# Products of two k tiles by turns, with weights at eight sets of places, and two raw weight buffers in place of three

## The chip, the core and the metric

The kernel runs on one core of one Trainium2 chip. The metric is the device time of a launch in microseconds (us). The time before is 2691.24 us, the median of 2 runs (2691.05 to 2691.44).

## What is computed

One inference step of a two-layer decoder, for a prompt of 256 tokens and 8 sequences of 8 new tokens each, 320 tokens in all, in float32. Layer 0 mixes tokens by gated linear attention (GLA), layer 1 by a chunked spatial gate; each is followed by a dense MLP with squared ReLU, and each sublayer by a residual LayerNorm:

```python
def sq_relu_mlp(x, w1, w2):
    return jnp.square(jax.nn.relu(x @ w1)) @ w2

for i in range(DEPTH):                     # DEPTH = 2
    if i % N_MIXERS == 0:
        h, s = gla_mixer(x, gla_w_in[j], ..., gla_w_out[j], gla_state0[j])
    else:
        h, v_rows = sg_mixer(x, sg_w_in[j], ..., sg_w_out[j])
    x = layer_norm(DEEPNORM_ALPHA * x + h, ln1_g[i], ln1_b[i])
    x = layer_norm(DEEPNORM_ALPHA * x + sq_relu_mlp(x, mlp_w1[i], mlp_w2[i]), ln2_g[i], ln2_b[i])
```

D_MODEL is 2048 and the MLP is 8192 wide. Nearly all the work is in the large products: `gla_w_in` (2048 x 6144 and a narrow gate part), `gla_w_out`, `sg_w_in`, `sg_w_out`, and for each layer `mlp_w1` and `mlp_w2`.

## The kernel before

**Three products for one.** Activations lie with the feature on the partition and the 320 tokens along it. A float32 operand is split in a high part, which is its value in the type float32r, and a low part, which is the rest. A weight tile w times an activation tile x becomes three TensorE products into one PSUM tile: low weights by high x (line 161), high weights by low x (L162), high weights by high x (L163). Each loads 128x128 weights and streams 320 columns (322 for a normalised input that carries two extra columns; those tiles are called dgh and dgl). The pairs of activation tiles are called xh/xl, oh/ol, yh/yl and hh/hl by stage.

**Units.** Weights come in units of 4 k tiles by 256 columns (512 KB), 736 in all. For a unit, `unit` issues a load into one of three buffers of the pool wraw (L138, on SyncE's queue, SP), lets ScalarE cast it into a high buffer wh (L144, ACT), and VectorE subtract to get the low buffer wl (L145, DVE). The first two units are loaded and split in pieces of one or two k tiles. The buffers wh and wl are taken in turn from a ring: ring a has four of each; from the end of the GLA layer on a ring b with four more of each joins, and units take the rings by turns. A unit's subtraction is what gives the raw buffer free; the last product of a unit gives its wh and wl free.

**Order of products.** `group` holds one PSUM tile for each 128 output columns, and for each unit does for both column halves n and the four k tiles kk the three products of `mm3`, in the order L161, L162, L163. The program is written in this order, and the scheduler of the tile framework then places the instructions of each engine by its own estimate of when they can start; small products of other work (attention heads, means) go in between.

**Places.** LINE is 64 floats, 256 bytes. The pools and a few unused fill tiles are laid out so that all wh tiles start at a multiple of 256 bytes in the partition; a gap tile of LINE // 4 floats (`Ring.part`) puts the wl tiles 64 bytes past one; and the big activation tiles start LINE // 2 floats, 128 bytes, into a line (`bigtile`). A row of a weight unit is 1024 bytes and a half of it 512, and a k tile of 320 activations is 1280 bytes, so these places within 256 bytes are the same for each k tile and each half. Only the dgh and dgl tiles, with 322 columns, have a different place for each k tile.

**The start.** The input x is loaded in pieces (L225, half of a quarter at a time, xr) on the same SP queue as the weights; the loads of the gate's weights (L293 into wgr, L296 into wgr2) stand there too. The narrow gate product of the GLA layer is L316 and L317: for each k tile one weight tile, taken twice, by xl and by xh. Its 16 weight tiles follow each other in steps of 512 bytes.

## Time and profile before

| | |
|---|---|
| median of the timed runs | 2691.24 us |
| profiled execution, first to last instruction (span) | 2689.4 us |
| TensorE clock granted, mean | 1.000 of full |
| DMA, mean over the span | 165 GB/s, 442.42 MB |
| weight loads on SP's queue | 512 KB each, 3.5 to 4.5 us from issue to landing in the median |
| SP's queue waiting for a raw buffer (L138 <- DVE wl L145) | 2150.6 us, 692 times |

The profile names an engine, the line of the kernel, the tiles (out<-in, buffer numbers left out), the number of instructions, then the busy time, the mean duration of one in ns, and the idle time of the engine before them with what ended it. PE is TensorE, PEld its weight loads. Matmuls overlap in the records: one of 128x320 lasts some 300 ns there, while the next starts much earlier, so the busy share of TensorE says little, and the distance from start to start is what counts. Durations of a stretch are given as min/median/max where a single line is asked for.

### The profile page before, as it was taken

What the parts mean: (1) busy time and instruction counts of PE and PEld (TensorE: products, weight loads), DVE (VectorE), ACT (ScalarE), POOL (GpSimd) and SP (SyncE); (2) the same over time, 40 slices, a digit from 0 to 9 for tenths busy, and PEclk for the clock granted to TensorE, in tenths of its full rate; (3) what the DMA queues carried; (4) which work ended last, traced back from release to release, by engine and by line L of the source; (5) the groups of instructions that cost most, each with busy time, mean ns of one, the idle gap of its engine ahead of it and who ended that gap; (6) DMA issues with size and microseconds to landing.
All of it is one profiled execution on the core that took longest, in us unless ns stands there. A gap on an engine that the chain in (4) does not pass through costs nothing.

```text
span 2689.4 us, 44906 instructions
## 1 busy us (share of the span) xinstructions
PE 2680.7 (100%) x18395; PEld 2658.8 (99%) x18395; DVE 1550.3 (58%) x2322; ACT 1162.5 (43%) x1638; POOL 226.4 (8%) x391
## 2 busy tenths in 40 slices
PE   9999999999999999999999999999999999999999
PEld 9999999999999999999999999999999999999998
DVE  7677677885444444444478776686444444444446
ACT  5455455564334334333446554355334333333434
POOL 4353341000000000000001032000000000000000
PEclk9999999999999999999999999999999999999999
DMA  8667667545445545444445555455445444454552
GB/s 252 220 196 249 217 198 253 189 142 159 155 150 155 151 150 156 150 153 152 150 152 161 157 158 149 134 165 153 153 150 156 150 152 154 150 155 150 152 154 79
DMA packets 138494, 442.42 MB, mean 165 GB/s; under 512 B 20912, under 2 KB 27952, under 8 KB 138288
## 3 DMA queue, kind: packets, MB, share of 16 engines
q1 hardware_dynamic: 121440, 408.08, 49.2%
q0 software_dynamic: 16304, 30.82, 3.7%
q8 instruction: 144, 2.36, 0.4%
q10 hardware_dynamic: 544, 0.66, 0.1%
q14 instruction: 62, 0.51, 0.1%
HBM read 409.60 MB, written 22.02 MB: 160 GB/s over the span
## 4 chain that ended last, share of the span: by engine, by line
PE 99%; DMA 0%; ACT 0%; DVE 0%; ACTq 0%; issue 0%; DVEq 0%
PE mm L161 32%; PE mm L163 32%; PE mm L162 31%; PE gl L631 1%; PE gl L634 1%; PE gl L589 1%; PE gl L1003 0%; PE gl L573 0%; DMA raw<-gla_w_in 0%; ACT z L1087 0%; DMA xr<-xT 0%; PE gl L558 0%; PE gl L603 0%; PE gl L574 0%; PE gl L552 0%; PE gl L1004 0%
## 5 line engine op out<-in xcount | busy, mean ns | idle before, releaser
L145 DVE TENSOR_TENSOR wl<-raw,wh 128x1024 fp32r<-128x1024 f32 (+1 forms) x740 | 902.3, 1220 | 953.2 <-ACT wh L144 950.9
L144 ACT CAST wh<-raw 128x1024 fp32r<-128x1024 f32 (+1 forms) x740 | 771.5, 1044 | 1251.9 <-PE mm L163 1127.1
L163 PE MATMUL mm<-yh,wh 128*128 128x320 f32 x2624 | 805.9, 307 | 0.0
L161 PE MATMUL mm<-yh,wl 128*128 128x320 f32 x2624 | 803.2, 309 | 0.0
L162 PE MATMUL mm<-yl,wh 128*128 128x320 f32 x2624 | 794.9, 303 | 0.0
L161 PE MATMUL mm<-hh,wl 128*128 128x320 f32 x2048 | 631.5, 308 | 0.0
L163 PE MATMUL mm<-hh,wh 128*128 128x320 f32 x2048 | 629.0, 307 | 0.0
L162 PE MATMUL mm<-hl,wh 128*128 128x320 f32 x2048 | 619.9, 303 | 0.0
L162 PEld LDWEIGHTS mm<-yl,wh 128*128 128x128 f32 x2624 | 492.7, 188 | 0.0
L163 PEld LDWEIGHTS mm<-yh,wh 128*128 128x128 f32 x2624 | 491.4, 187 | 0.0
L161 PEld LDWEIGHTS mm<-yh,wl 128*128 128x128 f32 x2624 | 491.0, 188 | 0.0
L161 PEld LDWEIGHTS mm<-hh,wl 128*128 128x128 f32 x2048 | 384.6, 188 | 0.0
L162 PEld LDWEIGHTS mm<-hl,wh 128*128 128x128 f32 x2048 | 384.6, 188 | 0.0
L163 PEld LDWEIGHTS mm<-hh,wh 128*128 128x128 f32 x2048 | 383.4, 187 | 0.0
L161 PE MATMUL mm<-xh,wl 128*128 128x320 f32 x768 | 238.2, 311 | 1.4 <-DVE wl L145 0.7
L163 PE MATMUL mm<-xh,wh 128*128 128x320 f32 x768 | 236.4, 309 | 0.0
L162 PE MATMUL mm<-xl,wh 128*128 128x320 f32 x768 | 235.2, 306 | 0.0
L161 PEld LDWEIGHTS mm<-xh,wl 128*128 128x128 f32 x768 | 144.1, 188 | 5.4 <-DVE wl L145 1.0
L162 PEld LDWEIGHTS mm<-xl,wh 128*128 128x128 f32 x768 | 144.3, 188 | 4.4 <-issue 1.2
L163 PEld LDWEIGHTS mm<-xh,wh 128*128 128x128 f32 x768 | 143.7, 187 | 2.6 <-issue 0.7
L1053 POOL CAST ident_r<-ident 128x128 fp32r<-128x128 f32 x1 | 0.3, 286 | 1027.9 <-PE gl L772 1027.9
L936 POOL DMA_DIRECT2D bsp<-sg_wT x1 | 0.6, 558 | 999.7 <-PE mm L163 999.7
(265 smaller groups left out, 2380.3 us busy)
## 6 DMA issues: line engine op xcount, KB each, us to landing
raw<-mlp_w SPq DMA_DIRECT2D x512, 512.0 KB, 3.5
raw<-gla_w_in SPq DMA_DIRECT2D x94, 512.0 KB, 4.1
raw<-sg_w_in SPq DMA_DIRECT2D x64, 512.0 KB, 3.6
st<-state SPq DMA_DIRECT2D x32, 512.0 KB, 5.7
o_state_s<-st POOLq DMA_DIRECT2D x32, 512.0 KB, 4.2
raw<-gla_w_out SPq DMA_DIRECT2D x32, 512.0 KB, 4.5
raw<-sg_w_out SPq DMA_DIRECT2D x32, 512.0 KB, 3.5
va<-blk POOLq DMA_DIRECT2D x128, 32.0 KB, 4.3
```

Source lines behind the costliest of these rows:

```text
L144: nc.scalar.copy(hi[:, ks, :], raw[:, ks, :])
L145: nc.vector.tensor_sub(lo[:, ks, :], raw[:, ks, :], hi[:, ks, :].bitcast(F32))
L161: nc.tensor.matmul(ps, wl[:, kk, s], x_h, start=first, stop=False)
L162: nc.tensor.matmul(ps, wh[:, kk, s], x_l, start=False, stop=False)
L163: nc.tensor.matmul(ps, wh[:, kk, s], x_h, start=False, stop=last)
L589: nc.tensor.matmul(pairs(pu), hd.ktp[:, kt, blk, :], hd.v_prompt(blk), start=(blk == 0), stop=(blk == 1))
L631: nc.tensor.matmul(po[:], qm[:, kt, b * P : (b + 1) * P], part[:], start=False, stop=(b == DB - 1 and kt == 1 and part is sth))
L634: nc.tensor.matmul(pairs(pu), kz[:, i, kt, g, :], hd.v_sample(g), start=True, stop=True)
L936: nc.gpsimd.dma_start(wsT, A["sg_wT"])
L1053: nc.gpsimd.tensor_copy(ident_r[:], ident[:])
```

## The change

`Ring.part` and `mm3` go. A new class `Weights` is a tile with its own map from k tile to offset: even k tiles start at one place in a line, odd ones at another. High and low tiles each get LINE more floats. `Ring.parts` gives the buffers of a ring, four in turn, one of four sets of places and an order of products; with two rings there are eight. `Q` is LINE // 4 floats, 64 bytes; `at(even, odd)` takes the two places in units of Q. An order is a list of six products for an even and an odd k tile: (0 or 1 for the k tile, "lh" for low weights by high x, "hl" for high weights by low x, "hh" for both high). The pool wraw has two buffers. Casts and subtractions write two runs of 512 floats for a whole unit instead of one of 1024.

```diff
+class Weights:
+    def __init__(self, tile, base, a, b):
+        self.tile, self.base, self.a, self.b = tile, base, a, b
+    def row(self, k):
+        return self.base + k // 2 * self.a + k % 2 * self.b
+    def put(self, ks):
+        k, n = ks.start, ks.stop - ks.start
+        if n == 1:
+            return self.tile[:, self.row(k) : self.row(k) + UN].rearrange("p (a b n) -> p a b n", a=1, b=1)
+        one = self.tile[:, self.row(k) : self.row(k) + 1]
+        return bass.AP(tensor=one.tensor, offset=one.offset,
+                       ap=[list(one.ap[0]), [self.a, n // 2], [self.b, 2], [1, UN]])
...
+Q = LINE // 4
+TURNS = ((0, "lh"), (0, "hl"), (1, "hl"), (1, "lh"), (1, "hh"), (0, "hh"))
+TURNS_LAST = ((0, "lh"), (0, "hl"), (1, "hl"), (0, "hh"), (1, "hh"), (1, "lh"))
+SWAPPED = tuple((1 - k, p) for k, p in TURNS)
+PLAIN = tuple((k, p) for k in range(2) for p in ("lh", "hl", "hh"))
+BOTH_LOW = ((0, "lh"), (0, "hl"), (1, "lh"), (1, "hl"), (0, "hh"), (1, "hh"))
+def at(even, odd):
+    return even * Q, UN, 2 * UN + (odd - even) % 4 * Q
+PLACES = {
+    "a": [(at(0, 1), at(1, 0), TURNS), (at(0, 3), at(3, 0), TURNS),
+          (at(0, 1), at(1, 0), TURNS_LAST), (at(0, 0), at(1, 1), PLAIN)],
+    "b": [(at(0, 3), at(1, 0), TURNS), (at(3, 0), at(0, 3), SWAPPED),
+          (at(0, 0), at(1, 1), BOTH_LOW), (at(1, 0), at(0, 1), SWAPPED)],
+}
 class Ring:
...
-        t = self.pool.tile([P, UK, UN], F32R, tag=p + self.tag, name=name)
-        if not self.gap:
-            self.pool.tile([P, LINE // 4], F32, tag="gap", name=name + "_gap", bufs=1)
-            self.gap = True
-        return t
+    def parts(self, hi, lo):
+        *at, order = PLACES[self.tag][self.turn % 4]
+        self.turn += 1
+        h, l = (Weights(self.pool.tile([P, UK * UN + LINE], F32R, tag=p + self.tag, name=n), *x)
+                for p, n, x in zip("hl", (hi, lo), at))
+        return h, l, order
...
-    wraw = ctx.enter_context(tc.tile_pool(name="wraw", bufs=3))
+    wraw = ctx.enter_context(tc.tile_pool(name="wraw", bufs=2))
...
-            nc.scalar.copy(hi[:, ks, :], raw[:, ks, :])
-            nc.vector.tensor_sub(lo[:, ks, :], raw[:, ks, :], hi[:, ks, :].bitcast(F32))
-        return hi, lo
+            src = raw[:, ks, :].rearrange("p (a b) n -> p a b n", b=min(step, 2))
+            nc.scalar.copy(hi.put(ks), src)
+            nc.vector.tensor_sub(lo.put(ks), src, hi.put(ks).bitcast(F32))
+        return hi, lo, order
...
-    def mm3(ps, wh, wl, kk, n, rh, rl, k, c0, cn, first, last):
-        s = slice(n * P, (n + 1) * P)
-        x_h, x_l = rh[:, k, c0 : c0 + cn], rl[:, k, c0 : c0 + cn]
-        nc.tensor.matmul(ps, wl[:, kk, s], x_h, start=first, stop=False)
-        nc.tensor.matmul(ps, wh[:, kk, s], x_l, start=False, stop=False)
-        nc.tensor.matmul(ps, wh[:, kk, s], x_h, start=False, stop=last)
+    def product(ps, ws, kk, n, xs, k, pair, cn, first, last):
+        w, x = (o["hl".index(p)] for o, p in zip((ws, xs), pair))
+        nc.tensor.matmul(ps, w[:, kk, slice(n * P, (n + 1) * P)], x[:, k, 0:cn], start=first, stop=last)
...
                 for n in range(2):
-                    for kk in range(UK):
-                        k = q * UK + kk
-                        mm3(ps[2 * i + n][:], wh, wl, kk, n, rh, rl, k, 0, width, k == 0, k == KT - 1)
+                    prods = [(2 * a + b, pair) for a in range(UK // 2) for b, pair in order]
+                    for j, (kk, pair) in enumerate(prods):
+                        product(ps[2 * i + n][:], (wh, wl), kk, n, (rh, rl), q * UK + kk, pair, width,
+                                q == 0 and j == 0, q == NU - 1 and j == len(prods) - 1)
...
-        lp.tile([P, 3 * LINE // 4], F32, tag="fill", name="fill_l")
+        lp.tile([P, LINE], F32, tag="fill", name="fill_l")
```

On TensorE the change reorders the products within a unit. Before, in the second matmul of the last MLP chunk of layer 0, from one unit to the next (mm is the PSUM tile, hh and hl the activations, wh and wl the weights):

```order
L161 MATMUL mm_14368<-hh_12567,wl_14371 128x320
L162 MATMUL mm_14368<-hl_12568,wh_14370 128x320
L163 MATMUL mm_14368<-hh_12567,wh_14370 128x320
L161 MATMUL mm_14367<-hh_12567,wl_14401 128x320
L162 MATMUL mm_14367<-hl_12568,wh_14400 128x320
L163 MATMUL mm_14367<-hh_12567,wh_14400 128x320
```

Here now, in the same matmul, from a unit in the order TURNS to the next:

```order
L202 MATMUL mm_14502<-hh_12565,wl_14505 128x320
L202 MATMUL mm_14502<-hl_12566,wh_14504 128x320 x2
L202 MATMUL mm_14502<-hh_12565,wl_14505 128x320
L202 MATMUL mm_14502<-hh_12565,wh_14504 128x320 x2
L202 MATMUL mm_14501<-hh_12565,wl_14535 128x320
L202 MATMUL mm_14501<-hl_12566,wh_14534 128x320 x2
L202 MATMUL mm_14501<-hh_12565,wl_14535 128x320
L202 MATMUL mm_14501<-hh_12565,wh_14534 128x320 x2
```

The products of two k tiles stand interleaved: the two by low x follow each other, and so do the two by both high parts, with the low weights of the odd k tile between them.

On SP's queue at the start, before (raw_155 and raw_201 are the first two units' loads, raw_242 and raw_272 the third's and fourth's; xr are pieces of x, wgr the gate's weights):

```order
L138 DMA raw_155<-gla_w_in 128x512 x2
L138 DMA raw_201<-gla_w_in 128x512 x2
L225 DMA xr_234<-xT 128x2x320
L225 DMA xr_236<-xT 128x2x320
L138 DMA raw_242<-gla_w_in 128x1024
L293 DMA wgr<-gla_w_low 128x256
L225 DMA xr_302<-xT 128x2x320
L138 DMA raw_272<-gla_w_in 128x1024
```

And now (the third and fourth units' loads are raw_241 and raw_271):

```order
L179 DMA raw_155<-gla_w_in 128x512 x2
L179 DMA raw_200<-gla_w_in 128x512 x2
L265 DMA xr_233<-xT 128x2x320
L265 DMA xr_235<-xT 128x2x320
L333 DMA wgr<-gla_w_low 128x256
L336 DMA wgr_340<-gla_w_gate 16x1024
L265 DMA xr_301<-xT 128x2x320
L179 DMA raw_241<-gla_w_in 128x1024
L336 DMA wgr_340<-gla_w_gate 16x1024 x2
L265 DMA xr_303<-xT 128x2x320
L336 DMA wgr_340<-gla_w_gate 16x1024 x2
L179 DMA raw_271<-gla_w_in 128x1024
```

The third unit's load has moved behind the gate's first two loads and a piece of x, the fourth's behind four more gate loads and the next piece of x.

## The prediction

> **What bounds the kernel now.** I read the page first: busy time, granted clock, and the chain that ended last.

> ```profile
> span 2689.4 us, 44906 instructions
> ...
> PE 2680.7 (100%) x18395; PEld 2658.8 (99%) x18395; DVE 1550.3 (58%) x2322; ACT 1162.5 (43%) x1638; POOL 226.4 (8%) x391
> ...
> PE 99%; DMA 0%; ACT 0%; DVE 0%; ACTq 0%; issue 0%; DVEq 0%
> ```

> TensorE is never idle, and the chain is TensorE alone. So the time is the number of products times their spacing, from start to start. A busy PE says nothing of that spacing, so I took it from a stretch of the MLP part (busy time by stretch: span, TensorE with its matmuls counted in brackets, weight loads, the other engines, and behind them the granted clock, 1.00).

> ```profile
> 760.00:1450.00 690.00, 690.00 (x4777) 690.00 (x4776) 342.41 (x428) 262.62 (x336) 0.00 (x0) 1.00 0.50 152
> ```

> 690.00 / 4777 = 144.4 ns. The three products of a k tile are not alike, though all are 128x320. The first three rows below are groups by line (last numbers: busy us, mean ns of one); the fourth is the chain inside 900 to 1400 us, where each line has 1154 or 1155 products.

> ```profile
> L161 PE MATMUL mm<-hh,wl 128*128 128x320 f32 x2048 | 631.5, 308 | 0.0
> L163 PE MATMUL mm<-hh,wh 128*128 128x320 f32 x2048 | 629.0, 307 | 0.0
> L162 PE MATMUL mm<-hl,wh 128*128 128x320 f32 x2048 | 619.9, 303 | 0.0
> ...
> by line: PE mm L161 33.9%; PE mm L163 33.3%; PE mm L162 32.7%; PE gl L795 0.0%
> ```

> By the chain the spacings are 0.339 x 500 / 1154 = 146.9 ns for L161, 144.3 for L163 and 141.7 for L162. One nanosecond more of recorded duration goes with about one more of spacing, so durations can be read as spacings: the quick product is L162, the one right after the low weights.

> **What the change does to that.** It alters neither the number nor the size of the products, only their order and where in a line of 256 bytes (the kernel's LINE) the weights lie. By the tile sizes the moving parts start 128 bytes into a line, before and after. Before, low weights start 64 bytes in and high weights at 0, so the place read goes 64, 0, 0, 64, 0, 0. After, six of the eight variants change place at every product (64, 0, 64, 0, or 192, 0, 192, 0, or both mixed). One is the old order at the old places. One changes at four of six products and holds at two (both low products first).

> Is it the change of place that makes a product quick? Two stretches speak to that. The first has sixteen products whose weights never change place (L316 and L317, the low gate); the row of 23.08 is the product behind them. The last row is a stretch at 601 us where the scheduler put five L162 behind L163, high weights at 0 each time.

> ```profile
> 20.73 0.31 PE L316 MATMUL gl<-xl,wgp 128*128 128x320 f32 x1
> ...
> 23.08 0.31 PE L161 MATMUL mm<-xh,wl 128*128 128x320 f32 x1
> ...
> L162 PE MATMUL mm<-yl,wh x5: 308/308/308, 600.5 to 601.7; 128*128 128x320 f32 x5
> ```

> A place held costs (23.08 - 20.73) / 16 = 146.9 ns, and L162 loses its quickness (308 in place of 303). So a change of place does save something: about 2.5 ns a product in the old pattern, which changes twice in three. Does changing at each product save more? At one place in each of three heads the scheduler left out an L163, and the places ran 64, 0, 64, 0. That is the change's pattern, four products long:

> ```profile
> 258.10 0.31 PE L161 MATMUL mm<-xh,wl 128*128 128x320 f32 x1
> 258.25 0.30 PE L162 MATMUL mm<-xl,wh 128*128 128x320 f32 x1
> 258.39 0.31 PE L161 MATMUL mm<-xh,wl 128*128 128x320 f32 x1
> 258.54 0.31 PE L162 MATMUL mm<-xl,wh 128*128 128x320 f32 x1
> 258.68 0.31 PE L163 MATMUL mm<-xh,wh 128*128 128x320 f32 x1
> ...
> L162 PE MATMUL mm<-xl,wh x2: 305/306/307, 152.7 to 153.0; 128*128 128x320 f32 x2
> ```

> The four take 258.68 - 258.10 = 0.58 us, 145.0 ns each, no better than 144.4; and in the same pattern at 152.7 us the first L162 takes 305 and the second 307, not 303. The quickness wears off when every product is to have it. I take 145.0 for the alternating variants. Bounds: 141.7 below (every product as quick as L162) and above the dearest rows of this kind, those whose moving parts lie at all places:

> ```profile
> L161 PE MATMUL mm<-dgh,wl 128*128 128x322 f32 x192 | 59.6, 311 | 0.0
> L163 PE MATMUL mm<-dgh,wh 128*128 128x322 f32 x192 | 59.6, 310 | 0.0
> ```

> With these 310 or so against a mean of 306 they stand 4 ns above 144.4, less about 0.9 for two more columns: 147.5; L161's 311 leads to 148, which I take as the upper bound. No row shows weights at 192; I price them as those at 64.

> The units: 736 of 24 products. Ring a serves the first 104 alone, then every other one: 420; ring b 316. Alternating: 3/4 of each, 552 units, 13,248 products at +0.56 ns (145.0 - 144.44) = +7.4 us. Both-low: 79 units, 1,896 products, four of six at 145.0 and two at 146.9, 145.6 in the mean, +2.3 us. Old order: 105 units, nothing.

> [...]

> **Two raw buffers.** A raw buffer is taken from its load's issue to the end of the subtraction. Rows of 700 to 1400 us: landing (min, median, max), cast, subtraction.

> ```profile
> DMA to landing us min/median/max: 3.3/3.5/5.3
> ...
> L144 ACT CAST wh<-raw x202: 1036/1048/1059, 699.3 to 1397.5; 128x1024 fp32r<-128x1024 f32 x101
> ...
> L145 DVE TENSOR_TENSOR wl<-raw,wh x201: 1224/1227/1237, 700.3 to 1399.2; 128x1024 fp32r<-128x1024 f32 x101
> ...
> ACT wh L144 <- PE mm L163: 1127.1, 514, 3.8
> ```

> 3.5 + 1.05 + 1.23 = 5.8 us a turn, and two buffers have two units, 2 x 24 x 144.4 = 6.9 us. So it is hidden, with 1.1 us to spare where there were 4.6; and the cast mostly waits for TensorE to leave a ring buffer (last row), so several finished units stand in front of TensorE and cover single late landings. Casts and subtractions now take two broken runs of 512 in place of one of 1024; the kernel's own split of x in broken runs, the next row, costs 820 ns for 640, in line with 1227 for 1024, so I add nothing. If that cover were gone, conversions 1.1 us longer would begin to set TensorE's pace; at twice their length a turn is 8.1 us, 0.6 us too much a unit, some 350 us in 600 units.

> ```profile
> L231 DVE TENSOR_TENSOR xl<-xr,xh 128x640 fp32r<-128x640 f32 x6 | 4.9, 820 | 0.1
> ```

> The start has no units in front. Its rows: landing over the first 30 us, the issues of the third and fourth unit's loads, and TensorE's first product of the third unit.

> ```profile
> DMA to landing us min/median/max: 3.5/5.9/7.2
> ...
> 4.97 0.34 SPq L138 DMA_DIRECT2D raw<-gla_w_in  x1
> ...
> 7.06 0.33 SPq L138 DMA_DIRECT2D raw<-gla_w_in  x1
> ...
> 13.68 0.42 PE L161 MATMUL mm<-xh,wl 128*128 128x320 f32 x1 [0.73 <-DVE wl L145]
> ```

> The third load now waits for the first unit's buffer, which is what the fourth's issue at 7.06 waited for: 2.1 us later, and the order moves it behind the gate's loads and an x load on SP's queue. TensorE already waited for this unit's subtraction (0.73 us of idle time at 13.68), so 2.1 us or more go straight onto the path. The fourth and fifth loads slip likewise; behind them in SP's queue wait x loads, and the first matmuls of the next k tiles wait for those. I take 4.5 us in all, between 2.1 (the third load alone) and 7.2 (one whole landing of the longest kind).

> **Sum.** 7.4 + 2.3 + 4.5 = +14.2 us on the span of 2689.4: 2703.6. The timed runs (median 2691.24) lie 1.8 above the span: 2705.

> **Rivals.**
> 1. Every change of place is quick: 141.7 for alternating products (-36.3), 143.4 for both-low (-2.0), start +4.5: 2657. For it: 303 against 308 after a change. Against it: the 305 and 307 when changes follow on each other.
> 2. Place does not matter: +4.5 alone, 2696. [...] Against it: the 308 of L162 with its place held.
> 3. Alternation settles to the price of a held place, 146.9: (13,248 + 1,896) x 2.46 = +37.3, start +4.5: 2733. For it: 307 after 305, still rising.
> 4. Slower by over 2%: alternating at 192 and 64 meets the moving parts as badly as the rows of all places do, 148: 15,144 x 3.56 = +53.9, +4.5: 2749.6. It decides from 147.7 ns up. Against it: no row with whole 64-byte places is that dear.
> 5. Conversions or landings pass 6.9 us a turn and starve TensorE, as priced above.

> **How the numbers follow.** My forecast 0.38, rival 1 0.20, rival 2 0.15, rival 3 0.14, rival 4 0.06, rival 5 0.02; 0.05 for a spacing below 140.6, which no row shows and which alone would be over 2% faster. The range from 2652 to 2740 holds the forecast and rivals 1 to 3 and leaves 0.13 out. Taking 2%, about what a measurement can tell: faster 0.05, within 0.87, slower 0.08.

> **What would show it.** In the changed profile: 4777 products in about 693 us of the same stretch; the products by turns near 306 to 308, none at 303 throughout; TensorE's third unit starting 2 to 3 us later, and hardly a wait of TensorE after 30 us. Wrong would be: alternating products at 303 (rival 1), at 310 or more (rival 4), or a row of TensorE waiting for the subtraction in the middle of the program (rival 5).

## The result, and the profile after

The changed kernel takes 2733.87 us (median of 2 runs, 2733.51 to 2734.23) against 2691.24: 1.0158 times the kernel before, 95% interval 1.0129 to 1.0188. It is slower by 42.6 us. The forecast was 2705; the time is that of the third rival, 2733, and as the experiments show, not quite for that rival's reasons.

The page first: span, busy time, and the chain that ended last by engine and by line.

```profile
span 2731.8 us, 44892 instructions
...
PE 2717.9 (99%) x18395; PEld 2692.9 (99%) x18395; DVE 1552.4 (57%) x2322; ACT 1164.8 (43%) x1638; POOL 226.5 (8%) x391
...
PE 91%; DMA 4%; DVE 3%; ACT 2%; issue 0%; ACTq 0%; DVEq 0%; POOLq 0%
```

TensorE still looks full, but the chain is no longer TensorE alone: 9% of it now runs on other engines and loads, most of it loads, casts and subtractions of weights, which had 0% before. So two things have to be looked for: dearer products, and waits for weights. The products first, in the stretch that the prediction named (busy time by stretch, TensorE's matmuls in the first brackets, granted clock third from the end).

```profile
760.00:1450.00 690.00, 690.00 (x4718) 690.00 (x4717) 330.93 (x405) 256.47 (x323) 0.00 (x0) 1.00 0.48 149
```

Nothing waits there, and the clock is full, yet 4718 products pass in place of 4777: 146.25 ns each in place of 144.44. The groups by line (busy us, mean ns of one) show no quick product any more; high weights by the low part hl, 303 ns before, now take 307:

```profile
L202 PE MATMUL mm<-hh,wl 128*128 128x320 f32 x2048 | 609.5, 308 | 0.0
L202 PE MATMUL mm<-hl,wh 128*128 128x320 f32 x2048 | 503.2, 307 | 0.0
L202 PE MATMUL mm<-hh,wh 128*128 128x320 f32 x2048 | 486.5, 308 | 0.0
```

These groups mix eight variants. The timeline of TensorE (start us, us, operation) takes them apart: the first two rows are 18 products apart in a unit that changes place at each product, the rest belongs to a unit in the old order.

```profile
1009.32 0.45 PE L202 MATMUL mm<-hh,wh 128*128 128x320 f32 x2
...
1011.96 0.45 PE L202 MATMUL mm<-hh,wh 128*128 128x320 f32 x2
...
1015.92 0.31 PE L202 MATMUL mm<-yh,wl 128*128 128x320 f32 x1
1016.07 0.30 PE L202 MATMUL mm<-yl,wh 128*128 128x320 f32 x1
...
1019.38 0.31 PE L202 MATMUL mm<-yh,wl 128*128 128x320 f32 x1
```

Alternating: (1011.96 - 1009.32) / 18 = 146.7 ns. Old order: (1019.38 - 1015.92) / 24 = 144.2 ns, with the quick 0.30 back at once. From the start times of all products after 600 us, sorted by the variant of their buffer (start of the next product minus own start, gaps over 200 ns left out):

| Variant | products | ns each |
|---|---|---|
| a: turns 0/64; turns 0/192; turns_last | 1795; 1770; 1768 | 146.66; 146.67; 146.58 |
| a: old order | 1771 | 144.57 (147.5, 140.2, 145.8) |
| b: turns 192/64 mixed; swapped 192; swapped 64 | 1774; 1772; 1764 | 146.72; 146.69; 146.77 |
| b: both low | 1774 | 146.46 |

Six variants stand at 146.6 to 146.8, which is where a place that is held will turn out to stand in the experiments (146.6). And the waits: TensorE's in the first 30 us, then behind them (engine, line, what it waited for: us in all, times, longest).

```profile
PE mm L202 <- DVE wl L187: 2.5, 1, 2.5
```

```profile
PE mm L202 <- DVE yl L862: 2.5, 2, 1.3
PE mm L202 <- DVE nw L227: 0.7, 1, 0.7
```

There were none after 30 us before. What lies behind them is on ScalarE, in the heads: its waits from 30 to 440 us, in the kernel before and in the changed one.

```profile
ACT wh L144 <- PE mm L163: 98.7, 56, 3.6
...
ACT wh L144 <- DMA raw<-gla_w_in: 5.5, 2, 2.8
```

```profile
ACT wh L186 <- DMA raw<-gla_w_in: 57.6, 31, 3.8
...
ACT wh L186 <- PE mm L202: 49.3, 28, 4.9
```

Before, the cast waited for a ring buffer, with the raw weights long there; now it waits for the weights 31 times. The start of units (counted from 0) in the two traces says where each loss falls:

| Start of unit | 2 | 10 | 110 | 130 | 140 | 150 | 200 | 735 |
|---|---|---|---|---|---|---|---|---|
| before, us | 13.68 | 46.58 | 482.62 | 552.24 | 588.06 | 622.80 | 796.14 | 2668.93 |
| changed, us | 15.87 | 50.75 | 492.71 | 563.18 | 605.01 | 640.15 | 815.75 | 2711.72 |
| behind | 2.2 | 4.2 | 10.1 | 10.9 | 16.9 | 17.4 | 19.6 | 42.8 |
| behind, less 1.8 ns a product | 2.1 | 3.7 | 5.3 | 5.3 | 10.9 | 10.9 | 10.9 | 11.0 |

From unit 200 on only the spacing differs: 23.2 us in 535 units, 1.8 ns a product. At that rate the 735 units give about 32 us, and about 11 us are left for the two raw buffers, all of them lost before unit 200. The last row says where: 3.7 us up to unit 10, 1.6 more up to the end of the heads, and 5.6 between units 130 and 140, at the start of the first MLP. So in this kernel most of ScalarE's waits in the heads do not reach TensorE.

The waits are not all of it. The granted clock (third number from the end) fell to a half twice, right behind a stretch in which TensorE was mostly idle:

```profile
13.77:17.16 3.39, 1.29 (x9) 1.29 (x10) 3.23 (x4) 1.93 (x3) 0.00 (x0) 1.00 1.04 279
17.18:20.58 3.40, 3.40 (x15) 3.40 (x14) 2.95 (x4) 3.06 (x5) 0.00 (x0) 0.50 0.73 269
...
594.03:597.43 3.40, 1.34 (x5) 0.82 (x6) 3.40 (x7) 2.92 (x6) 0.00 (x0) 1.00 0.50 155
597.45:600.84 3.39, 3.39 (x14) 3.39 (x14) 3.39 (x8) 2.62 (x5) 0.00 (x0) 0.50 0.55 166
600.86:604.25 3.39, 3.39 (x25) 3.39 (x24) 3.39 (x8) 1.49 (x3) 0.00 (x0) 1.00 0.53 180
```

In a stretch at half clock 14 or 15 products pass in place of 25, which is 1.5 us or so. The two make about 3 of the 11 us.

### The profile page after: what moved, and what is told of

Its sections match the earlier page's. It is cut to its first block, busy times and chain, and to the rows that moved or that the text cites. A ratio compares the mean times of both kernels' runs of the same rounds, so it can differ in the third digit from the quotient of the medians.

```text
span 2731.8 us, 44892 instructions
## 1 busy us (share of the span) xinstructions
PE 2717.9 (99%) x18395; PEld 2692.9 (99%) x18395; DVE 1552.4 (57%) x2322; ACT 1164.8 (43%) x1638; POOL 226.5 (8%) x391
## 4 chain that ended last, share of the span: by engine, by line
PE 91%; DMA 4%; DVE 3%; ACT 2%; issue 0%; ACTq 0%; DVEq 0%; POOLq 0%
PE mm L202 87%; DMA raw<-gla_w_in 2%; DVE wl L187 1%; DMA raw<-gla_w_out 1%; PE gl L671 1%; ACT wh L186 1%; DMA raw<-mlp_w 1%; PE gl L674 1%; PE gl L629 1%; DMA z<-xT 0%; PE gl L1043 0%; PE gl L613 0%; ACT z L1127 0%; DVE dgl L817 0%; DVE t L857 0%
## 5 line engine op out<-in xcount | busy, mean ns | idle before, releaser
L202 PE MATMUL mm<-yl,wh 128*128 128x320 f32 x2624 | 647.2, 308 | 2.7 <-DVE yl L862 2.5
L202 PE MATMUL mm<-yh,wh 128*128 128x320 f32 x2624 | 624.5, 309 | 0.0
L202 PE MATMUL mm<-hl,wh 128*128 128x320 f32 x2048 | 503.2, 307 | 0.0
L202 PE MATMUL mm<-hh,wh 128*128 128x320 f32 x2048 | 486.5, 308 | 0.0
L202 PEld LDWEIGHTS mm<-yl,wh 128*128 128x128 f32 x2624 | 451.7, 188 | 3.5 <-DVE yl L862 3.4
L202 PEld LDWEIGHTS mm<-yh,wh 128*128 128x128 f32 x2624 | 445.7, 188 | 0.0
L202 PEld LDWEIGHTS mm<-hh,wh 128*128 128x128 f32 x2048 | 347.4, 187 | 0.0
L202 PE MATMUL mm<-xl,wh 128*128 128x320 f32 x768 | 194.7, 312 | 0.0
L202 PE MATMUL mm<-xh,wh 128*128 128x320 f32 x768 | 193.4, 310 | 0.0
L928 ACT CAST hh<-f 128x320 fp32r<-128x320 f32 x128 | 58.6, 459 | 69.8 <-DVE f L927 69.8
```

What stands on the lines that cost most here:

```text
L202: nc.tensor.matmul(ps, w[:, kk, slice(n * P, (n + 1) * P)], x[:, k, 0:cn], start=first, stop=last)
L928: nc.scalar.copy(hh[:, j, 0:T], f[:])
```

## The experiments

All of them run beside the kernel before; ratios are to it.

### Two raw buffers alone

```diff
-    wraw = ctx.enter_context(tc.tile_pool(name="wraw", bufs=3))
+    wraw = ctx.enter_context(tc.tile_pool(name="wraw", bufs=2))
```

> The kernel before with two raw buffers and nothing else. In the changed profile the spacing of its products accounts for 13,248 x 2.22 + 1,896 x 2.0 = 33 us of the 42.6 us that it lost (146.67 and 146.45 ns against 144.45). Theory 1, two raw buffers cost the other 9 us (the start and a few late conversions): about 2700. Rival, they cost the 4.5 us of the prediction and something else of the change costs the rest: about 2696. Rival, nothing: 2691.

Measured: 2711.09 us (2709.28 to 2711.99), ratio 1.0073 (1.0060 to 1.0085). All three expectations were too low. The third buffer is worth 20 us by itself, over four times what the prediction gave it.

### The old order and places in the new code

```diff
+PLACES = dict.fromkeys("ab", [(at(0, 0), at(1, 1), PLAIN)] * 4)
```

> The changed kernel with all eight variants set to the old order and the old places. Theory 1 (two raw buffers are all that is left): the same time as the kernel before with two raw buffers, about 2700, and three products in 433.3 ns. Rival, the conversions in two broken runs cost something too: some us more than that kernel. Rival, eight different variants side by side disturbed each other: then this is below it.

Measured: 2708.80 us (2705.11 to 2711.03), ratio 1.0068 (1.0054 to 1.0082). With its runs overlapping those of the kernel before with two raw buffers, no price of the broken runs shows, and as many products pass in the stretch of 760 to 1450 us as before:

```profile
760.00:1450.00 690.00, 690.00 (x4778) 690.00 (x4778) 336.96 (x413) 259.20 (x328) 0.00 (x0) 1.00 0.49 152
```

So beside the places and the raw buffers no third cause shows.

### A held place

```diff
+PLACES = dict.fromkeys("ab", [(at(0, 0), at(0, 0), PLAIN)] * 4)
```

> The old order, but low and high weights at place 0 in all buffers, so that the place never changes; hl and hh still use the same weights one after the other. Theory P (the sequence of places sets the spacing; a held place costs 146.67): 17,664 x 2.22 = 39 us above the kernel with the old places, about 2740, all three products of a k tile near 308 ns. Rival S (the product is quick because its successor uses the same weights again, which the by-turns order gave up): 2700, with one product in three at 303.

### The order by turns at the old sequence of places

```diff
+PLACES = dict.fromkeys("ab", [(at(0, 0), at(1, 1), TURNS)] * 4)
```

> The by-turns order in all buffers, but high weights at 0 and low ones at 64 in even and odd k tiles alike, so that the places run 64, 0, 0, 64, 0, 0 as in the kernel before while no product uses its predecessor's weights. Theory P (places): 144.4 ns a product, about 2700, as the old order. Rival S (same weights again): 146.67 ns, about 2740. Rival M (the order xh, xl, xh of the moving parts, here xh, xl, xl, xh, xh, xh, sets it): 2740 or between.

Measured: the held place 2740.22 us, ratio 1.0181 (1.0167 to 1.0195); the order by turns 2710.62, ratio 1.0073 (1.0059 to 1.0086). The same stretch as above, of the first, and then of the second:

```profile
760.00:1450.00 690.00, 690.00 (x4707) 690.00 (x4706) 329.58 (x402) 254.49 (x322) 0.00 (x0) 1.00 0.48 149
```

```profile
760.00:1450.00 690.00, 690.00 (x4779) 690.00 (x4779) 335.19 (x410) 259.39 (x327) 0.00 (x0) 1.00 0.49 152
```

This pair decides between order and place. With the order unchanged and the place held, products slow to 146.6 ns (690.00 / 4707); with the by-turns order, other neighbours, other weights one after the other, but the places still 64, 0, 0, they stay at 144.4, 1.5% less. Theories S and M fall; theory P stands: the sequence of places sets the spacing, not which product follows which. (It does not always set it to one value; two exceptions stand further below.)

### A held place with three raw buffers

```diff
-        if not self.gap:
+        if p == "l" and not self.gap:
```

The gap of 64 bytes now lies behind the low tiles, which start at place 0 as the high ones.

> The kernel before, three raw buffers and its own order, with low weights moved to place 0 as the high ones: only the place is held. Theory P: 17,664 x 2.22 = 39 us above the kernel before, 2730, with nothing of the wait at the start. Rival (the price of places shows in full only where two raw buffers starve the conversions): near 2691.

Measured: 2726.96 us (2726.89 to 2727.30), ratio 1.0134 (1.0117 to 1.0151). This is the price of places with no wait in it, in the same stretch as above:

```profile
760.00:1450.00 690.00, 690.00 (x4706) 690.00 (x4706) 332.98 (x407) 255.97 (x325) 0.00 (x0) 1.00 0.48 150
```

The price is 36 us for all products, a little under the 39 expected. About 1 us of the difference is that the 576 products of dgh and dgl, whose own place moves, lose only 0.4 ns each (147.8 to 148.2 by start times). The changed kernel slows 15,144 of its 17,664 products: 0.857 x 35.9 = 31 us, in line with the 32 above. It also shows an interaction: two raw buffers cost 20 us on quick products, but 2740.22 - 2726.96 = 13.3 where the place is held. The granted clock has a part in it: in the profiled runs it fell to a half three times with quick products (from 17, 468 and 601 us on) and once with the held place (from 16 us on), which makes some 3 us of difference. The rest is open; that dearer products leave the conversions more time is only an argument.

### Sixteen pairs of places

```diff
+PAIRS = [(h, l) for h in range(4) for l in range(4)]
...
+        h, l = PAIRS[unit_no[0] % 16]
...
+                          *at(x, x)) for p, n, x in zip("hl", (hi, lo), (h, l))), PLAIN)
```

> The changed kernel with the old order in all units, and sixteen pairs of places by turns: high weights 0, 64, 128 or 192 bytes into a line (a, b, c, d), low weights at any of the four, so that the sequence is lo, hi, hi with every step. The marks stand in the tiles' names (whab: high at a, low at b). Theory P1 (any change of place that is followed by a hold makes one product quick): the twelve unequal pairs have one product in three near 303 ns and 144.4 ns in the mean, the four equal pairs none and 146.7. Rival P2 (only the step from a place to the one below counts): ba-like pairs (lo one above hi) are quick, the others at 146.7 or above. Rival P3 (the place against that of the moving part at 128 counts): pairs with the same step differ. A pair below 140 ns in the mean would be a better layout than the kernel's own.

The one run took 2736.21 us, but a mixture's own time means little; the rows do. High weights by low yl (mean ns of one): first the widest step (high d, low a), then a held place, the reversed pair ba, and the old pair ab.

```profile
L198 PE MATMUL mm<-yl,whda 128*128 128x320 f32 x176 | 54.8, 311 | 0.0
...
L198 PE MATMUL mm<-yl,whaa 128*128 128x320 f32 x152 | 47.1, 310 | 0.0
...
L198 PE MATMUL mm<-yl,whba 128*128 128x320 f32 x152 | 46.7, 307 | 0.0
...
L198 PE MATMUL mm<-yl,whab 128*128 128x320 f32 x152 | 46.2, 304 | 0.0
```

By start times (ns, from a unit's first product to its 24th, over 23, in the units whose products follow each other without a break): ab 144.98, db 145.44, bc 145.54, bd 145.84, ba 145.91, ca 145.94, cb 146.11; ac, ad, cd, dc 146.66 to 146.80; da 147.29; the four equal pairs 146.66 to 146.89. P1 falls: five of twelve unequal pairs save nothing. P2, which means ab where its text says ba, falls too: ab, bc and cd all step down by one place, and cd gains nothing. P3, that the pair's absolute place counts, is what is left. These means hide that a pattern takes time to settle: by the groups of three products of a unit in order, ca has 148.95, 147.64, 145.57 and 148.30, and then 144.43, 144.45 and 144.45 (the eighth and last borders on the next pair). So ca settles level with the old pair, and no pair settles below it.

### All 256 combinations, and sixteen sequences held for long

The first mixes them unit by unit (one run of 2728.90 us), the second holds each for 46 units (2725.87 us).

```diff
+        v = unit_no[0] * 37 % 256
...
+SEQS = ["bbcc", "bcTT", "dbad", "acTT", "acba", "aabb", "caab", "bdab",
+        "acda", "bbdc", "bdTT", "bdbb", "acbc", "cbaa", "cdTT", "dabb"]
...
+        mark = SEQS[min(unit_no[0] // 46, 15)]
```

> As the sixteen pairs, but even and odd k tiles have their own places: all 256 combinations of places for high and low weights of even and odd k tiles, each in two or three units. By P1 a product's spacing depends on whether its place differs from that of the product ahead and equals that of the next, whatever the k tile. If steps add up, some sequence of steps lies below the 144.4 ns of 64, 0, 0; if the saving can be had once in three products at most, none does.

> Sixteen sequences of places, each held for 46 units in a row so that it runs settled; letters a to d are the places 0, 64, 128, 192, in the order high even, high odd, low even, low odd (aabb is the kernel before). Twelve are in the old order; four (TT) are the by-turns order between two places. In the mixed run of 256, acba had 144.5 ns and caab 144.8 where aabb had 145.0. Theory A (sums of steps differ): settled, acba goes below 144.45, to 143.8 or less, and alternations between other pairs of places need not sit at 146.67. Rival B (144.45 is the least that any sequence settles to): acba and caab settle at 144.4 to 144.8, and all four TT at 146.67.

In the mixture the means run from 144.65 (acba) to 148.04 ns (aaac). Held for long, three sequences have the same spacing to the hundredth. Busy time by stretches of 145 us: first acTT, then acba, aabb (the kernel before) and caab, and last cdTT.

```profile
610.00:755.00 145.00, 145.00 (x1002) 145.00 (x1001) 73.77 (x94) 59.39 (x81) 0.00 (x0) 1.00 0.50 153
770.00:915.00 145.00, 145.00 (x1006) 145.00 (x1005) 68.00 (x79) 56.73 (x74) 0.00 (x0) 1.00 0.49 153
930.00:1075.00 145.00, 145.00 (x1006) 145.00 (x1006) 64.35 (x71) 50.23 (x58) 0.00 (x0) 1.00 0.49 152
1090.00:1235.00 145.00, 145.00 (x1006) 145.00 (x1005) 63.66 (x70) 48.22 (x55) 0.00 (x0) 1.00 0.50 152
...
2390.00:2535.00 145.00, 145.00 (x991) 145.00 (x989) 62.20 (x68) 47.73 (x53) 0.00 (x0) 1.00 0.47 149
```

By start times: acba, aabb, caab 144.44 each; bdab, bdbb, cbaa, dabb 145.55 to 145.56; acbc and cdTT 146.67. Rival B holds in its main point: none of the sequences tried goes below 144.44. Its last clause fails: alternation between 0 and 128 (acTT) has 145.0, and between 64 and 128 (bcTT) 145.3. Between 64 and 192 (bdTT) it has two values. Up to 1809 us it stands at 145.0; then the dgh and dgl products of the next product group pass, and behind them it goes to 146.4 to 146.7, with the weights at the same places:

```profile
1745.00:1800.00 55.00, 55.00 (x382) 55.00 (x380) 44.68 (x81) 28.27 (x45) 0.00 (x0) 1.00 0.46 140
1845.00:1900.00 55.00, 55.00 (x377) 55.00 (x377) 37.44 (x62) 30.59 (x50) 0.00 (x0) 1.00 0.47 146
```

So alternation is not dear as such. Those that the change chose are dear in the mixture in which the change has them; none of them was held for long by itself.

### The moving part at other places

```diff
+X_LOW = [1, 1, 0, 0, 0, 0, 0, 1, 3, 3, 3, 3, 3]
...
-        start = LINE // 2 if width == T else 0
+        start = place * Q if width == T else 0
```

> The old order with the sixteen pairs of places for high and low weights, eight units each in turn, and the low moving part (xl, ol, yl, hl) no longer at 128 beside the high one: at 64 in the first part and in the spatial gate, at 0 in the first MLP, at 192 in the second. Theory A (the place of the moving part against the weights counts too, so that a step of the moving part can be traded for one of the weights): some pair settles below the 144.44 ns that is the least of all sequences so far. Rival B (144.44 is a floor, whatever reads where): none does; equal pairs may become quick, since the moving part now steps. Rival C (the moving part's place does not count): the table of pairs is that of the run with all moving parts at 128, ab at 144.4 to 145.0 and equal pairs at 146.67.

One run, 2741.51 us. Rows of the second MLP, low moving part at 192 (1900 to 2700 us): the old pair against a pair that holds its place at 192.

```profile
L199 PE MATMUL mm<-hl,whab 128*128 128x320 f32 x128 | 39.5, 309 | 0.0
...
L199 PE MATMUL mm<-yl,whdd 128*128 128x320 f32 x128 | 39.2, 306 | 0.0
```

Both are high weights by a low moving part (hl or yl). The old pair has lost its quick product and a held place gained some. By start times, the best pair with the low moving part at 0 is bd, 145.56; at 64 it is cc, which settles at 144.4; the worst is ba at 64, 150.3. At 192 cc has 144.46 in the eight units from 2215 us on and 147.4 in those from 2666 us on, behind the first of them, with order and places the same. Its low weights by high hh in the two stretches:

```profile
L199 PE MATMUL mm<-hh,wlcc 128*128 128x320 f32 x59 | 17.8, 303 | 0.0
...
L199 PE MATMUL mm<-hh,wlcc 128*128 128x320 f32 x57 | 17.7, 310 | 0.0
```

Rival C falls: the place of the moving part counts too, since a pair that holds its place at 146.66 to 146.89 ns with all moving parts at 128 reaches 144.4 (cc) when the moving part steps. Rival B holds again. So no version came out of this that beats both kernels: the kernel before already stands on the least spacing found.

### Where the third raw buffer is needed

First with two raw buffers up to the end of the heads and three behind, then the converse:

```diff
+        pools = [wraw, wraw, wr2] if wr2 else [wraw]
+        raw = pools[units[0] % len(pools)].tile([P, UK, UN], F32, tag="raw", name=nm("raw"))
```

> The kernel before with two raw buffers up to the end of the heads and three from there on. Theory (what two raw buffers cost by the gaps of TensorE in the trace of that run: 3.6 us in the first 30 us, 4.4 in the heads, 8.3 from 460 to 600 us, 1.6 behind it): the last two go and 2691 + 10 = 2701 is left. Rival (the wait from 460 to 600 us comes of the load queue having fallen behind in the heads): it stays at 2709 to 2711.

> The kernel before with three raw buffers up to the end of the heads and two from there on, the converse of three later. By TensorE's progress in the profiled runs, two raw buffers throughout are 14.3 us behind at the start of unit 110 (497.0 us against 482.6 before) and lose 6 more up to unit 150. Theory (the two losses are separate; the first is the heads', the second that of the stage behind them, 460 to 600 us): the first goes, 2691 + 6 = 2697. Rival (the second is a consequence of the first: the loads arrive there already late): about 2691.

Measured: three only later 2709.56 us (2705.41 to 2711.74), ratio 1.0067 (1.0052 to 1.0082); three only early 2693.18 us (2692.73 to 2694.81), ratio 1.0008 (0.9999 to 1.0017). The first missed its 2701: taking the loss in the heads from the gaps between products had counted too little of it; why is not shown. In its trace unit 110 starts 14.4 us late and unit 150 is no later. The second settles it: of the 20 us that two raw buffers cost the kernel before, 18 come of having only two up to the end of the heads. Its waits of ScalarE from 30 to 440 us are those of the kernel before again:

```profile
ACT wh L146 <- PE mm L165: 104.4, 58, 4.0
...
ACT wh L146 <- DMA raw<-gla_w_in: 2.7, 1, 2.7
```

Behind the heads it loses 2 us where two buffers throughout lost 6, so part of that loss is a consequence of the one in the heads; that TensorE arrives there with little in hand is only an argument.

### Work in the start's wait

```diff
+                if units[0] == 2:
+                    spare = gltile(T)
+                    for _ in range(14):
+                        nc.tensor.matmul(spare[:], wl[:, UK - 1, 0:P], rh[:, UK - 1, 0:T], start=True, stop=True)
```

This adds 14 products that nothing reads.

> The kernel before with two raw buffers, and 14 spare products (into a bank that nothing reads) between the second and the third unit, about 2.06 us of work in TensorE's 2.5 us wait there. Theory (the granted clock of 0.66 from 16 to 21 us, products at 267 ns, follows from the idle time): the third unit's products run at 145 ns, TensorE's start is 2 us shorter, about 2709. Rival (the clock falls for another reason, such as the load on the chip at that time): products at 267 ns all the same, and 2711.

The stretch from 16 to 21 us, with two raw buffers alone, and then with the spare products:

```profile
16.00:21.00 5.00, 5.00 (x24) 5.00 (x25) 4.52 (x5) 4.09 (x7) 0.00 (x0) 0.66 0.85 253
```

```profile
16.00:21.00 5.00, 4.99 (x34) 5.00 (x35) 4.25 (x5) 3.86 (x7) 0.00 (x0) 1.00 0.80 249
```

The clock stays full, and 34 products pass in place of 24. The time is 2708.59 us (2705.59 to 2710.34), ratio 1.0062 (1.0046 to 1.0079): some 2 us lower, but the runs overlap. They differ in the clock too: the runs of 2705.59 and 2707.58 us have a mean granted clock of 1.000, those of 2709.61 and 2710.34 of 0.998, and in the profiled one, of 2709.61, it stands at 0.50 from 464.1 to 467.4 and from 597.2 to 604.0 us. Unit 5 starts no earlier (30.40 us against 29.95): the narrow gate's products move forward (the first at 19.61 us against 21.07), and from 21 to 30 us 64 products pass in both.

## Why the prediction was right or wrong

**The sum.** It gave +14 us, and 42.6 were measured. The range held the time because it reached up to the third rival, not because the sum was near.

**The bound: right in the main.** TensorE's spacing decides about 32 of the 42.6 us, and a nanosecond of spacing is 17.7 us. (The quick product is 140.2 ns by start times, not the 141.7 that was read from the chain's shares; the mean of the three is the same. In the trace of before it is 140.0 ns for high by hl and 147.5 for low by hh, so that the 5 ns between their durations, 303 and 308, went with 7.5 of spacing.)

**"I take 145.0 for the alternating variants": the step that failed.** They settle at 146.67. So the first term, +7.4, measures 13,248 x (146.67 - 144.45) = 29.4 us, and the both-low term, +2.3, measures 1,896 x 2.0 = 3.8. The rows were read rightly in kind, 307 after 305, wearing off, and wrongly in size: four products and a pair were taken for the settled state, though the prediction's third rival said that they were still rising. The changed trace shows the same start of the pattern and what comes behind it: where a both-low unit follows one in the old order (68 units after 600 us), its first four products, at 64, 0, 64, 0, have 147.6, 141.2, 147.7 and 145.1 ns, 145.4 in the mean; from the fifth on the unit has 146.7. The held place at 146.9 was right within 0.3, and so were, in these alternations, the places at 192, priced as 64. The old-order variant at nothing was right (144.57).

**"Is it the change of place that makes a product quick?": only half.** The sequence of places decides (held place and order by turns, above). But it isn't change as such: five of twelve unequal pairs gain nothing (146.66 to 147.29 ns), and with the moving part elsewhere a held place gains (cc at 64, 144.4). The first rival (every change quick) would have needed that rule.

**"So it is hidden": the second step that failed.** The raw buffers were costed from rows of 700 to 1400 us, 5.8 us a turn against 6.9, and only the start was given a price, +4.5. The third unit's start was right (+2.2 for 2.1), and the start as a whole nearly so (3.7 us up to unit 10). What was put at nothing is 7 us behind it, 1.6 up to the end of the heads and 5.6 at the start of the first MLP. The rows of the heads were not used: there casts and subtractions share their engines with other work (from 30 to 440 us of the changed trace VectorE is busy for 69% and ScalarE for 50%, from 760 to 1450 us for 48% and 37%), and a turn from a load's issue to the end of its subtraction is 8.6 us in the median of units 3 to 99 of the changed trace, up to 15 (each unit's load issue and subtraction end), where units follow each other every 4.48 us and two buffers so have 8.95. (Part of a turn can be waiting for a ring buffer; the 31 casts that waited for a load are what shows the shortage.) So TensorE probably came into the first MLP with few finished units in hand. The experiment with three buffers early fits, on quick products: there the loss behind the heads is 2 us in place of 6. "Hardly a wait of TensorE after 30 us" failed too. Late casts and subtractions also hold up what stands behind them on ScalarE and VectorE; the timeline of the changed kernel:

```profile
593.73 1.05 ACT L186 CAST wh<-raw 128x1024 fp32r<-128x1024 f32 x1 [1.19 <-DMA raw<-mlp_w]
...
594.35 0.55 PE L202 MATMUL mm<-yl,wh 128*128 128x320 f32 x2 [1.19 <-DVE yl L862]
...
594.69 0.56 ACT L859 ACTIVATE yh<-t,vec 128x320 fp32r<-128x320 f32 x1
...
595.30 0.56 PE L202 MATMUL mm<-yh,wl 128*128 128x320 f32 x2 [0.40 <-ACT yh L859]
```

The cast waits for a load, the activation behind it for the cast, and TensorE for the activation. The larger wait, 1.19 us at 594.35, is for the low part yl from VectorE, which had a subtraction of weights in front of it from 592.21 to 593.43 us. Neither these waits nor the half clock behind them was in any term.

**The rivals.** The second, that place does not matter, is refuted by the held place alone (146.6 ns against 144.4). The third has the right cause (the alternations settle at 146.67 ns, a held place at 146.6), and its 2733 is within 1 us of the measured time, but its terms are not: 37.3 for the places, where about 32 were measured, and 4.5 for the raw buffers, where it was about 11. The two errors cancel. The fifth (starving) came true in a small form, at the start of the first MLP.

## What to carry to other kernels

A pattern's price is that of its settled state: take it from dozens of repetitions, not from the first few (here a pattern took four to twelve products to settle), and if the trace has only a few, let the rising row decide. Cost a buffer in the stage where its engines are busiest, not where its rows are cleanest. And when a total comes out right, check the terms apart: here two errors of 5 and 6.5 us met.

## What the runs showed of the hardware that was not expected

The commonest settled spacings lie in steps: 144.44, 145.00, 145.56 and 146.67 ns are 866.7, 870.0, 873.3 and 880.0 ns for six products, multiples of 3.33 apart. One sequence can settle on more than one of them: bdTT stood at 145.0 and, behind other products, at 146.7; cc with the low moving part at 192 at 144.46 and at 147.4. What holds it there is open. One product by itself goes down to 140.0 ns (high by low in aabb, acba and caab). The spacing depends on more than the neighbours: in the mixture of 256, the places of a product and of its two neighbours explain 18% of the variance of its spacing, those of six products in a row 48% (means of 64 and of 1,142 groups of 16,924 products; so fine a grouping would explain some 7% by chance).

In the kernel with two raw buffers alone, TensorE's start after 2.46 us of waiting:

```profile
15.92 0.42 PE L161 MATMUL mm<-xh,wl 128*128 128x320 f32 x1 [2.46 <-DVE wl L145]
...
17.46 0.47 PE L161 MATMUL mm<-xh,wl 128*128 128x320 f32 x1
...
20.13 0.47 PE L162 MATMUL mm<-xl,wh 128*128 128x320 f32 x1
```

From 17.46 to 20.13 pass ten products, 267 ns each. With the spare products the slow stretch did not come. But in the new code with the old order (two raw buffers too) TensorE idled longer, and the clock stayed full:

```profile
16.27 0.41 PE L197 MATMUL mm<-xh,wl 128*128 128x320 f32 x1 [3.39 <-DVE wl L182]
```

So the length of the wait alone does not decide. The records of the granted clock show more. In every trace all its changes lie whole multiples of 3.41 us apart (with two raw buffers alone at 6.92, 17.16, 20.57, 467.72, 471.13, 600.84 and 604.25 us), so in each run they lie on a grid of such windows, at a place of its own. Here are the windows around the wait, first with two raw buffers alone, then in the new code with the old order (behind the stretch its length, then TensorE's busy time):

```profile
13.75:17.15 3.40, 1.23 (x8) 1.23 (x9) 2.96 (x4) 2.00 (x3) 0.00 (x0) 1.00 1.04 272
17.17:20.56 3.39, 3.39 (x15) 3.39 (x14) 3.20 (x4) 2.99 (x5) 0.00 (x0) 0.50 0.78 283
...
11.16:14.55 3.39, 1.72 (x12) 1.46 (x11) 2.48 (x4) 1.54 (x3) 0.00 (x0) 1.00 1.08 290
14.57:17.96 3.39, 1.69 (x11) 1.69 (x12) 2.63 (x4) 1.55 (x4) 0.00 (x0) 1.00 1.03 271
17.98:21.38 3.40, 3.40 (x26) 3.40 (x25) 3.23 (x3) 3.40 (x5) 0.00 (x0) 1.00 0.78 246
```
